# Low parts of the input weights on VectorE in place of GpSimd, and ACT table loads counted by the planner's clock, in a hybrid decoder step on one Trainium2 core

## The chip, the cores and the metric

The kernel runs on one core of one Trainium2 chip. The metric is the device time of one execution in microseconds (us), the median of three runs. The engines are named as the profile names them: PE (TensorE matmul), PEld (its weight loads), DVE (VectorE), ACT (ScalarE), POOL (GpSimd) and SP (SyncE, which here only issues DMAs).

## The reference

One layer of a decoder: two recurrent branches side by side, gated and merged, and then an MLP. It is computed for 512 prompt tokens and for 8 sequences of 4 sample tokens, so that a matrix of activations has 544 columns (552 where the 8 rows of an earlier state are appended). D is 1024, all data are float32.

```python
h = _rmsnorm(x, norm_mix_g)
u = h @ w_in                      # 1024 x 5888: [HGRN2 q,f,i,g | RWKV-7 r,k,v,loras | two gates]
o_a, s_a_new = _hgrn2_branch(...) # 4 heads, state 128x128, chunkwise gated recurrence
o_b, s_b_new = _rwkv7_branch(...) # 8 heads, state 64x64, delta-rule recurrence
x = x + (sigmoid(u_ga) * (o_a @ w_a_out) + sigmoid(u_gb) * (o_b @ w_b_out)) @ w_out
h2 = _rmsnorm(x, norm_mlp_g)
x = x + square(relu(h2 @ w_up)) @ w_down
y = _rmsnorm(x, norm_final_g)
```

The new states and the last normalised row are outputs too.

## The kernel before, in words

**Products.** A large product is made of three float32r products: each operand is split into a high part `hi` and a low part `lo = x - hi`, and hi·hi, lo·hi and hi·lo are added up in PSUM. `split` does this to a block of weights of 128x1024: ACT copies the staged block `st` into `whi`, and a second engine subtracts to make `wlo`. There are three buffers each for `st`, `whi` and `wlo`, so a later DMA of weights (SP's queue) waits until `wlo` of three blocks earlier has been made.

**Units.** The product h @ w_in is cut into 46 units of 128 columns of `w_in` (a token such as `k0`, `f1`, `G8`). A unit is 48 matmuls: two halves of the tokens, three products, 8 blocks of k. `ahead` loads the blocks of the next units and splits them; the variable `loaded` grows by one with each unit. The first 11 blocks are split with DVE, the others with POOL (`NDVE = 11`).

**Lanes.** Between the matmuls of the units stand the steps of the recurrences, in three lanes: LX (the RWKV-7 pairs 0/1, then 2/3: `rw_batch`, `rw_inverse`, `rw_solve`, `rw_affine`, `rw_chain`, `rw_out`), LZ (`low_rank`, `rw_values`, `rw_tokens`) and LY (`hg_head` 0 to 3, then `rw_state`, `rw_sample`, `hg_sample`). A lane is a generator; each `yield` ends one PE step. After every 4 matmuls (`FINE`) or 12 (`QUANT`) `gemm_h` calls `tick`, which goes on with each lane whose last step is ready by the planner's clock.

**The planner's clock.** `Clock` and `Timed` follow the program while it is emitted. Each instruction has a cost by its engine and size, and from the costs come the times at which tiles are ready. So the costs decide after which matmul of which unit a lane's next PE step is emitted. PE runs its instructions in exactly this order (`manual_schedule` for PE); the order on the other engines is set by a scheduler that works on data dependences. `choose` takes the next unit from a list of needed ones or from the gates (`FILL`), by the number of buffers that the lanes hold.

**After the units.** `drain(LX, LZ)` emits what is left in the lanes without matmuls of units between. Then come 8 half units (4 units' worth of matmuls) with `w_b_out`, with the rest of `hg_sample` between them, then those with `w_a_out`, which need the last result of `hg_sample` through DRAM (`oa_d`), then `w_out`, the MLP and the final norm. From `w_out` on PE is fed by large products alone.

Of the kernel before, what the change touches and what calls it, by code (L numbers as in the profile page):

```python
# [8 lines left out]
F32 = mybir.dt.float32  # L9
# [3 lines left out]
AF = mybir.ActivationFunctionType  # L13
ALU = mybir.AluOpType
# [30 lines left out]
PQ, LQ, ZQ, TQ = 0, 0, 1, 0  # L45
POOL_LO = 1
QUANT, FINE = 12, 4
NDVE = 11
NEED = "l0 k0 k1 r0 v0 r1 v1 l1 f0 q0 i0 g0 f1 q1 i1 g1 f2 q2 i2 g2 k2 k3 r2 r3 v2 v3 f3 q3 i3 g3"
FILL = "G8 G10 G2 G1 G3 G7 G13 G4 G11 G15 G9 G12 G5 G6 G14 G0"  # L50
X_WORK = "rw0 rw1"
# [70 lines left out]
class Timed:  # L122


    def __init__(self, eng, name, clock):
        self.eng, self.name, self.clock = eng, name, clock

    def cost(self, fn, out, ops, kw):
        n = 1
        for d in out.shape[1:]:  # L130
            n *= d
        big = max([n] + [int(o.free_size()) for o in ops if hasattr(o, "tensor")])
        if self.name == "PE":
            gemm = len(ops) > 1 and ops[1].dtype == F32R
            switch = 0.12 if gemm != self.clock.gemm else 0.0
            self.clock.gemm = gemm
            if gemm:
                return n / 2400 + 0.013 + switch
            if fn == "transpose":
                return 0.11 * max(n, 32) / 128 + switch  # L140
            return max(n, 32) * (0.00085 if ops[0].shape[-1] >= 128 or n >= 128 else 0.0006) + switch
        if fn == "dma_start":
            return 2.3
        if self.name == "V":
            if fn == "reciprocal":
                return 0.1 + 0.0064 * n
            if fn == "tensor_tensor_scan":
                return 0.1 + 0.0022 * n
            return 0.15 + 0.00106 * big
        if self.name == "A":  # L150
            return 0.17 + 0.0009 * big
        if fn == "tensor_tensor":
            return 0.2 + 0.0025 * big
        return 0.3 + 0.0012 * big
# [25 lines left out]
def hybrid_step(ctx: ExitStack, tc: tile.TileContext, i, o):  # L180
    nc = tc.nc
    clock = Clock()
    V, A, P, T = (Timed(e, n, clock) for e, n in ((nc.vector, "V"), (nc.scalar, "A"), (nc.gpsimd, "P"), (nc.tensor, "PE")))
# [73 lines left out]
    def tt(out, a, b, op, eng=None):  # L257
        (eng or V).tensor_tensor(out=out, in0=a, in1=b, op=op)
# [27 lines left out]
    class W:  # L286
        pass

    def split(st, eng=None):
        w = W()  # L290
        w.hi = pipe.tile([128, 1024], F32R, tag="whi", name=nm("whi"))
        w.lo = pipe.tile([128, 1024], F32R, tag="wlo", name=nm("wlo"), bufs=3)
        act(w.hi, st)
        tt(w.lo, st, w.hi.bitcast(F32), ALU.subtract, eng)
        return w

    def load8(src, c):
# [237 lines left out]
    def column(tok):  # L535
        n = int(tok[1:])
        if tok[0] in "lrkv":
            return B0 + 128 * ({"r": 0, "k": 4, "v": 8, "l": 12}[tok[0]] + n)
        return G0 + 128 * n if tok[0] == "G" else A0 + 512 * "qfig".index(tok[0]) + 128 * n

    need, fill, done, held, plan = NEED.split(), FILL.split(), set(), [0], []
    loaded, weights = {}, {column("l0"): pre}
# [13 lines left out]
    def ahead(c):  # L556

        for n, tok in enumerate(plan[0:3]):
            if tok not in loaded:
                loaded[tok] = load8(i["w_in"][0], column(tok))  # L560
        for tok in plan[0:2]:
            if tok in loaded and column(tok) not in weights:
                weights[column(tok)] = split(loaded[tok], P if len(loaded) > NDVE else V)
        return weights.pop(c)

    def in_unit(c, cuts=(0, HALF, TOK)):
# [30 lines left out]
    for kind in range(2):  # L597
# [3 lines left out]
        w = S(512, F32R, "lwd")  # L601
# [967 lines left out]
    while plan:  # L1569
        tok = plan.pop(0)  # L1570
# [58 lines left out]
    for jp in range(4):  # L1629
        if jp < 3:  # L1630
            wb.append(split(load4(i["w_b_out"][0], 256 * jp + 256)))
        w = wb[jp]
# [20 lines left out]
    for jp in range(4):  # L1653
        w = split(load4(i["w_a_out"][0], 256 * jp))
# [169 lines left out]
    for j in range(8):  # L1824
        st = load8(i["w_down"][0, 3072:4096], 128 * j)
        if j < 8 - NKEEP:
            w = []
# [54 lines left out]
```

## Time and profile before

| | us |
|---|---|
| median of 3 runs (lowest, highest) | 1102.83 (1100.08, 1108.12) |
| the profiled execution's own time | 1101.6 |
| its span, from the first to the last instruction | 1099.9 |

Busy time as a share of the span: PE 87%, PEld 84%, DVE 52%, ACT 37%, POOL 18%. The mean clock granted to PE is 0.937 of full speed. Of the chain of work that ended last, 62% is PE, 15% DVE, 7% DMA, 7% ACT, 4% POOL.

How to read it: PE is in order, so a lane's step that isn't ready holds up the matmuls behind it too. The units and lanes take the first 576 us of the span, the products with `w_b_out` and `w_a_out` go on to about 649 us, and the rest is PE-bound. What a step costs is therefore seen in the idle time of PE ahead of it, in brackets in the rows, with the engine and tile that ended it.

### The profile page before, as it was taken

How to read it: one execution, taken by the hardware profiler on the slowest of the kernel's cores; microseconds unless marked ns; L12 is line 12 of the kernel's file. 1: busy time of each engine (PE TensorE's matmuls, PEld its weight loads, DVE VectorE, ACT ScalarE, POOL GpSimd, SP SyncE). 2: the span in 40 equal slices, each digit the busy share in tenths (PEclk: the TensorE clock that was granted, in tenths of full speed). 3: DMA queues.
4: the chain of work that ended last, by engine and by line, in shares of the span. 5: the costliest groups of instructions: out<-in, count | busy, mean ns of one | idle time of the engine just before them, and what ended most of it. 6: DMA issues, size and time to landing. Idle time of an engine off the chain costs nothing.

```text
span 1099.9 us, 21956 instructions
## 1 busy us (share of the span) xinstructions
PE 957.2 (87%) x9220; PEld 923.6 (84%) x9220; DVE 577.3 (52%) x1135; ACT 404.9 (37%) x761; POOL 198.5 (18%) x335
## 2 busy tenths in 40 slices
PE   5887778798987879779949599999999999999996
PEld 4787767787887878769738599999999999999996
DVE  6464639445766585713566585544432234444533
ACT  7451524546444433433231234334311123332332
POOL 4267443222254442221010000000000000000000
PEclk9798788899998889989968799999999999999998
DMA  8421323221133233341265445332333323233411
GB/s 241 135 85 53 101 69 74 74 60 42 60 100 101 78 93 69 92 121 43 79 185 183 156 127 157 88 97 78 96 87 87 95 78 97 79 104 90 133 39 44
DMA packets 191093, 106.40 MB, mean 97 GB/s; under 512 B 38946, under 2 KB 179048, under 8 KB 190995
## 3 DMA queue, kind: packets, MB, share of 16 engines
q1 hardware_dynamic: 165424, 95.16, 29.6%
q10 hardware_dynamic: 25570, 9.85, 3.5%
q8 instruction: 72, 1.18, 0.4%
q14 instruction: 27, 0.21, 0.1%
HBM read 85.08 MB, written 18.39 MB: 94 GB/s over the span
## 4 chain that ended last, share of the span: by engine, by line
PE 62%; DVE 15%; DMA 7%; ACT 7%; POOL 4%; issue 4%; SPq 1%; ACTq 1%; POOLq 0%; DVEq 0%
PE pd L160 21%; PE full_unit_ps L160 14%; PE in_unit_ps L160 14%; PE half_unit_ps L160 3%; DVE tmp L160 2%; DMA st<-in_w_down_dram 2%; ACT whi L160 1%; POOL lmk L394 1%; DVE wlo L160 1%; ACT L160 1%; DVE X L160 1%; DVE rs L160 1%; DVE bn L160 1%; PE lora_ps L160 1%; SPq L160 1%
## 5 line engine op out<-in xcount | busy, mean ns | idle before, releaser
L160 ACT ACTIVATE whi<-st 128x1024 fp32r<-128x1024 f32 x120 | 126.8, 1056 | 267.9 <-PE pd L160 117.7
L160 DVE TENSOR_TENSOR wlo<-st,whi 128x1024 fp32r<-128x1024 f32 x85 | 104.1, 1225 | 65.9 <-ACT whi L160 65.8
L160 PE MATMUL in_unit_ps<-h_hi,wlo 128*128 128x272 f32 (+3 forms) x736 | 122.2, 302 | 0.0
L160 PE MATMUL in_unit_ps<-h_hi,whi 128*128 128x272 f32 (+3 forms) x736 | 117.7, 304 | 3.5 <-ACT h_hi L160 3.3
L160 PE MATMUL in_unit_ps<-h_lo,whi 128*128 128x272 f32 (+3 forms) x736 | 111.6, 295 | 0.0
L160 PE MATMUL full_unit_ps<-hd,whi 128*128 128x272 f32 (+2 forms) x832 | 109.8, 288 | 0.0
L160 PEld LDWEIGHTS in_unit_ps<-h_hi,whi 128*128 128x128 f32 x736 | 104.8, 200 | 5.4 <-ACT h_hi L160 3.8
L160 PEld LDWEIGHTS in_unit_ps<-h_hi,wlo 128*128 128x128 f32 x736 | 105.3, 197 | 2.0 <-issue 0.3
L160 PEld LDWEIGHTS full_unit_ps<-hd,whi 128*128 128x128 f32 x832 | 106.2, 188 | 0.0
L160 POOL TENSOR_TENSOR wlo<-st,whi 128x1024 fp32r<-128x1024 f32 x35 | 85.8, 2451 | 98.6 <-ACT whi L160 97.4
L160 PEld LDWEIGHTS in_unit_ps<-h_lo,whi 128*128 128x128 f32 x736 | 102.3, 195 | 0.1
L160 POOL TENSOR_SCALAR ys<-ys,ssf 32x512 f32<-32x512 f32 x1 | 1.1, 1087 | 532.8 <-DVE ssf L160 532.8
L160 DVE SCALAR_TENSOR_TENSOR r<-pd,rsb 128x272 f32<-128x272 f32 x64 | 25.2, 436 | 90.5 <-PE pd L160 89.1
L160 PE MATMUL pd<-xgh,wlo 128*128 128x272 f32 x512 | 70.1, 288 | 0.0
L160 PE MATMUL pd<-xgh,whi 128*128 128x272 f32 x512 | 69.8, 288 | 0.0
L160 PE MATMUL pd<-xgl,whi 128*128 128x272 f32 x512 | 69.6, 287 | 0.0
L160 PEld LDWEIGHTS pd<-xgh,wlo 128*128 128x128 f32 x512 | 66.4, 188 | 0.0
L160 PEld LDWEIGHTS pd<-xgh,whi 128*128 128x128 f32 x512 | 66.3, 188 | 0.0
L160 PEld LDWEIGHTS pd<-xgl,whi 128*128 128x128 f32 x512 | 66.2, 188 | 0.0
L160 DVE TENSOR_TENSOR x<-x,full_unit_ps 128x272 f32<-128x272 f32 (+2 forms) x48 | 19.5, 435 | 71.6 <-PE full_unit_ps L160 71.6
L160 PE MATMUL full_unit_ps<-hd,wlo 128*128 128x272 f32 (+2 forms) x416 | 56.5, 288 | 0.0
L160 PEld LDWEIGHTS full_unit_ps<-hd,wlo 128*128 128x128 f32 x416 | 53.8, 188 | 0.0
(414 smaller groups left out, 1558.9 us busy)
## 6 DMA issues: line engine op xcount, KB each, us to landing
st<-in_w_in_dram SPq DMA_DIRECT2D x46, 512.0 KB
st<-in_w_up_dram SPq DMA_DIRECT2D x32, 512.0 KB
st<-in_w_down_dram SPq DMA_DIRECT2D x32, 512.0 KB
gt_d<-gt SPq DMA_DIRECT2D x16, 272.0 KB
st<-in_w_out_dram SPq DMA_DIRECT2D x8, 512.0 KB
gtb<-gt_d SPq DMA_DIRECT2D x8, 272.0 KB
gta<-gt_d SPq DMA_DIRECT2D x8, 272.0 KB
x<-xt_d SPq DMA_DIRECT2D x8, 272.0 KB
```

The lines of the kernel that those rows point to most:

```text
L160: r = real(*a, **kw)
L394: return tc.keep_in_program_order(getattr(nc.gpsimd, name)(*a, **kw))
```

## The change

Two edits. `split` loses its argument for the engine, and `ahead` its test on `NDVE`: the low parts of blocks 12 to 46 of `w_in` are made on DVE, not on POOL. And the planner's cost of an ACT instruction is now 1.3 us higher where its function lies in another table set than the last one, and 0.2 us higher where it also writes a sum (`accum_out`). The second edit changes no instruction, but the order in which PE steps of lanes and units are emitted, and the order of units that `choose` makes.

```diff
-NDVE = 11
...
     def __init__(self, eng, name, clock):
-        self.eng, self.name, self.clock = eng, name, clock
+        self.eng, self.name, self.clock, self.table = eng, name, clock, 0
...
         if self.name == "A":
-            return 0.17 + 0.0009 * big
+            sets = {AF.Tanh: 1, AF.Exp: 1, AF.Sigmoid: 2, AF.Ln: 3, AF.Sqrt: 4}
+            new = sets.get(kw.get("func"), self.table)
+            load, self.table = 1.3 if new != self.table else 0.0, new
+            return 0.17 + 0.0009 * big + load + (0.2 if "accum_out" in kw else 0.0)
...
-    def split(st, eng=None):
+    def split(st):
...
-        tt(w.lo, st, w.hi.bitcast(F32), ALU.subtract, eng)
+        tt(w.lo, st, w.hi.bitcast(F32), ALU.subtract)
...
-                weights[column(tok)] = split(loaded[tok], P if len(loaded) > NDVE else V)
+                weights[column(tok)] = split(loaded[tok])
```

POOL around unit 12, before. `smk`, `bmk` and `mneg` are masks made by `consts3`, `sxl` is the low part of a product that PE sums over a head (`head_sums`).

```order
L394 MEMSET smk 128x64
L160 TENSOR_TENSOR wlo_1462<-st_1329,whi_1461 128x1024
L394 AFFINE_SELECT smk<-smk 32x32 x16
L394 MEMSET bmk 128x8
L394 AFFINE_SELECT bmk<-bmk 32x8 x8
L394 MEMSET mneg 128x1
L394 MEMSET mneg 32x1 x2
L160 TENSOR_TENSOR sxl_1484<-rk_1481,sxh_1483 128x544
```

The same place on POOL, now.

```order
L396 MEMSET smk 128x64
L396 AFFINE_SELECT smk<-smk 32x32 x16
L396 MEMSET bmk 128x8
L396 AFFINE_SELECT bmk<-bmk 32x8 x8
L396 MEMSET mneg 128x1
L396 MEMSET mneg 32x1 x2
L162 TENSOR_TENSOR sxl_1496<-rk_1493,sxh_1495 128x544
```

The block's low part `wlo_1462` no longer stands between the masks and `sxl`; on DVE it stands between two multiplications of the same pair's preparation.

PE at the solve of the pairs 2/3, before. `rw_state` transposes the sample states, `rw_solve_py` is the first step of `rw_solve`.

```order
L160 MATMUL rw_state_ps_5548<-ident,sn_5543 128x128 x4
L160 MATMUL in_unit_ps_5555<-h_hi,whi_5300 128x272 x8
L160 MATMUL in_unit_ps_5555<-h_hi,wlo_5301 128x272 x4
L160 MATMUL rw_state_ps_5585<-ident,sn_5568 128x128 x4
L160 MATMUL in_unit_ps_5555<-h_hi,wlo_5301 128x272 x4
L160 MATMUL in_unit_ps_5555<-h_lo,whi_5300 128x272 x8
L160 MATMUL rw_solve_py_5604<-XT_5573,zb_4550 32x32 x16
L160 MATMUL rw_solve_py_5604<-XT_5573,zb_4790 32x32 x16
L160 MATMUL in_unit_ps_5672<-h_hi,whi_5413 128x272 x8
L160 MATMUL in_unit_ps_5672<-h_hi,wlo_5414 128x272 x4
```

The same place on PE, now.

```order
L162 MATMUL rw_state_ps_5799<-ident,sn_5782 128x128 x4
L162 MATMUL in_unit_ps_5769<-h_hi,wlo_5543 128x272 x4
L162 MATMUL in_unit_ps_5769<-h_lo,whi_5542 128x272 x8
L162 MATMUL rw_solve_py_5818<-XT_5787,zb_4639 32x32 x16
L162 MATMUL rw_solve_py_5818<-XT_5787,zb_4997 32x32 x16
L162 MATMUL rw_state_ps_5858<-ident,sn_5853 128x128 x4
L162 MATMUL rw_solve_px_5869<-TT_5791,YT_5788 32x32 x16
L162 MATMUL rw_solve_px_5869<-TT_5796,YT_5788 32x32 x16
L162 MATMUL rw_sample_ps_5929<-rs_5907 64x64 x8
L162 MATMUL rw_sample_pt_5939<-ident,bd_5920 128x128 x4
L162 MATMUL rw_affine_pw_5946<-KA_5125,TT_5791 64x128 x8
```

Before, 192 matmuls of units (4 units) are left when the solve begins, and stand between its steps; now the last matmul of the last unit stands ahead of it.

PE at the end of `hg_sample`, before. `half_unit_ps` with `whi_6846` is the last block of `w_b_out`, with `whi_7091` the first of `w_a_out`.

```order
L160 MATMUL half_unit_ps_7010<-ol_6668,whi_6846 128x272
L160 MATMUL half_unit_ps_7010<-ol_6674,whi_6846 128x272
L160 MATMUL hg_sample_po_7023<-hs_6468,hs_6469 32x128 x4
L160 MATMUL hg_sample_pt_7050<-ident,hs_6468 128x128
L160 MATMUL half_unit_ps_7097<-oh_7067,whi_7091 128x272
```

The same place on PE, now. `whi_6812` is the last but one block of `w_b_out`, `whi_6898` the last.

```order
L162 MATMUL half_unit_ps_6972<-ol_6689,whi_6812 128x272
L162 MATMUL half_unit_ps_6972<-ol_6695,whi_6812 128x272
L162 MATMUL hg_sample_pt_6985<-ident,hs_6366 128x128
L162 MATMUL half_unit_ps_6997<-oh_6676,whi_6898 128x272
L162 MATMUL half_unit_ps_6997<-oh_6682,whi_6898 128x272
```

Before, `hg_sample_po` and `hg_sample_pt` follow one another behind the last matmul with `w_b_out`; now 36 matmuls stand between the two, and the 48 of the last block behind them.

## Rows read from the trace of the kernel before

**Rows 1.** Busy time by stretch: start:end, length, PE, PEld, DVE, ACT, POOL, PEclk, DMA.

```profile
125.00:488.00 363.00, 298.75 (x3611) 285.41 (x3611) 227.69 (x464) 155.69 (x316) 128.70 (x162) 0.92 0.29 79
```

**Rows 2.** What PE waited for from 125 to 488 us: total, times, longest.

```profile
PE hg_head_pt L160 <- DVE kh L160: 16.3, 4, 7.7
PE hg_head_pt L160 <- DVE hy L160: 16.1, 3, 8.2
PE head_sums_ps L160 <- POOL sxl L160: 6.9, 2, 6.2
PE rw_state_ps L160 <- DMA sn<-in_state_wkv_dram: 6.4, 1, 6.4
PE head_sums_ps L160 <- ACT sxh L160: 5.3, 1, 5.3
```

**Rows 3.** Groups of instructions: count, busy us, mean ns, idle time before and releaser.

```profile
L160 DVE TENSOR_TENSOR wlo<-st,whi 128x1024 fp32r<-128x1024 f32 x85 | 104.1, 1225 | 65.9 <-ACT whi L160 65.8
L160 POOL TENSOR_TENSOR wlo<-st,whi 128x1024 fp32r<-128x1024 f32 x35 | 85.8, 2451 | 98.6 <-ACT whi L160 97.4 <-POOL xi L160 1.0
L160 ACT ACT_TABLE_LOAD x19 | 24.4, 1283 | 2.3 <-PEq L1870 1.5 <-ACT gB L160 0.5
```

**Rows 4.** DVE in order of time, at four places from 132 to 506 us.

```profile
132.99 2.62 DVE L160 TENSOR_TENSOR eb<-kka,b 128x256 f32<-128x256 f32 x1
...
321.38 0.79 DVE L160 SCALAR_TENSOR_TENSOR xm<-d,prm,U 128x544 f32<-128x544 f32 x1
...
328.21 2.84 DVE L160 SCALAR_TENSOR_TENSOR xm<-d,prm,U 128x544 f32<-128x544 f32 x1 [2.87 <-POOL d L160]
...
504.41 2.10 DVE L160 TENSOR_TENSOR s0T<-s0T,rs 128x512 f32<-128x512 f32 x2 [1.04 <-PE rw_sample_pz L160]
```

**Rows 5.** POOL in order of time, 328 us.

```profile
328.13 2.34 POOL L160 TENSOR_TENSOR wlo<-st,whi 128x1024 fp32r<-128x1024 f32 x1
```

**Rows 6.** POOL in order of time, 132 to 146 us.

```profile
132.94 2.39 POOL L160 TENSOR_TENSOR wlo<-st,whi 128x1024 fp32r<-128x1024 f32 x1
...
144.04 1.33 POOL L160 TENSOR_TENSOR sxl<-rk,sxh 128x544 fp32r<-128x544 f32 x1
```

**Rows 7.** The chain that ended last, in order of time, a half unit: start, us, what.

```profile
231.12 3.21 PE in_unit_ps L160 x24
```

**Rows 8.** Busy time of the unit tiles alone, 488 to 542 us.

```profile
488.00:542.00 54.00, 27.83 (x192) 24.79 (x192) 0.00 (x0) 3.14 (x8) 1.00 0.19 64
```

**Rows 9.** Busy time by stretch, columns as in rows 1.

```profile
545.00:575.00 30.00, 14.37 (x188) 9.95 (x184) 18.66 (x61) 10.67 (x23) 2.75 (x9) 0.67 0.56 152
```

**Rows 10.** ACT in order of time, between the two steps of the solve and after.

```profile
489.42 1.21 ACT L160 ACTIVATE YT<-rw_solve_py 32x512 f32<-32x512 f32 x2
...
493.12 1.56 ACT L160 ACTIVATE TT<-rw_solve_px 32x256 f32<-32x256 f32 x4 [0.37 <-PE rw_solve_px L160]
```

**Rows 11.** DVE in order of time, first and last of the norm in `rw_sample`.

```profile
522.36 0.42 DVE L160 TENSOR_TENSOR rs<-rw_sample_pu,rs 128x256 f32<-128x256 f32 x1
...
529.01 0.42 DVE L160 TENSOR_TENSOR rs<-rs,gs 128x256 f32<-128x256 f32 x1
```

**Rows 12.** PE in order of time, two steps of `rw_chain` of pairs 2/3.

```profile
533.72 0.45 PE L160 MATMUL rw_chain_ps<-st,GQ 64*64 64x64 f32 x8
...
534.86 0.40 PE L160 MATMUL rw_chain_ps<-st,GQ 64*64 64x64 f32 x8
```

**Rows 13.** PE in order of time, `rw_out` of pairs 0/1 and of pair 2.

```profile
310.74 2.26 PE L160 MATMUL rw_out_pt<-ident,yo 64*64 64x64 f32 x64
...
560.93 1.97 PE L160 MATMUL rw_out_pt<-ident,yo 64*64 64x64 f32 x32
```

**Rows 14.** PE in order of time, 615 to 625 us.

```profile
615.67 0.45 PE L160 MATMUL hg_sample_pt<-ident,hs 128*128 128x128 f32 x1 [4.71 <-DVE hs L160]
622.50 2.42 PE L160 MATMUL half_unit_ps<-oh,whi 128*128 128x272 f32 x9 [6.38 <-ACT oh L160]
```

**Rows 15.** DVE in order of time, the first step of the second solve.

```profile
462.04 1.53 DVE L160 STREAM_TRANSPOSE XT<-D 32x256 f32<-32x256 f32 x4 [4.15 <-DMA D<-xz_d]
```

## The prediction

> **What bounds the kernel now.** I read the table of busy time by stretch first. From 125 to 488 us, where the lanes of both branches run between the units, PE is busy 299 of 363 us at a granted clock of 0.92 [rows 1], so 64 us are idle. The list of what PE waited for says on what: two of the steps of `hg_head` (`kh`, `hy`) for 16.3 and 16.1 us, the operands of `head_sums` (`sxl`, `sxh`) for 6.9 and 5.3, and a load of states (`sn`) for 6.4 [rows 2]: 51 of the 64 us in five rows. None of these is a wait for weights: no row has PE waiting for `wlo`. PE is in order, so a wait means that a lane's step was emitted before the chain on DVE, ACT and POOL behind it could be done. The engines themselves have room there, DVE with 228 us busy of 363, ACT 156, POOL 129. From 488 to 575 us the units' last 192 matmuls fill the gaps of the solve and the chain of the pairs 2/3 [rows 8]; then comes an uncovered end, 14.4 us busy of 30 at a clock of 0.67 [rows 9], and a second one at 610 to 622 us, where PE waits 4.7 us for the last norm of `hg_sample` and 6.4 us for its way through DRAM [rows 14]. Behind 649 us nothing changes: there PE is fed by large products alone.
>
> I work from the profiled execution, 1101.6 us, which lies 1.2 us below the median of the runs shown.
>
> **Part 1, the low parts.** 35 instructions go from POOL, at 2.451 us each, to DVE, at 1.225 us [rows 3]: 85.8 us less on POOL, 35 x 1.225 = 42.9 us more on DVE. But before, POOL's subtraction also held up DVE. An `xm` of 0.79 us took 2.84 us, and began 0.08 us behind a `wlo` of 2.34 us on POOL [rows 4, 5]. I went through DVE's instructions beside each of the 35: 24 of the 35 have one that is stretched, by 0.6 to 2.2 us over the common time of its form, from the `eb` at 133 us to the `s0T` at 504 us [rows 4], and the stretches add up to 39 us. So DVE gets back about 39 of the 43 us that it takes on, a net 4 us over 450, of which I put 2 us on the path. Bounds: if none of the stretch came back, up to 43 us of DVE work would be new, and at DVE's share of two thirds most of it would queue in front of a lane; if the stretch falls where lanes wait and the new work where DVE idles, up to 10 us are gained.
>
> The Trainium skill has the rule for such a stretch ("SBUF — State Buffer", section on the two separate sides): a GpSimd instruction and a VectorE instruction with two SBUF inputs take one shared pair of ports as an exclusive lock, and the one that comes second stands still for the whole of the other. The `xm` row agrees, a stretch of 2.05 us beside 2.34. The rule also speaks against the change, since `wlo` on DVE has two SBUF inputs and can now be held up by the POOL instructions that stay.
>
> What stays on POOL that is long are the eight `sxl`, 1.33 us each [rows 6]; 8 x 1.3 = 10 us if every one of them met a `wlo`, which 35 instructions of 1.2 us in 450 us will seldom do, so I take under 1 us, inside the 2 above. On the path POOL itself goes away at one place: `sxl` at 144 us stands behind a `wlo` of 2.39 us and 8 us of masks, and PE waits 6.2 us for it [rows 2, 6]. Without the `wlo` it is ready 2.4 us earlier.
>
> **Part 2, the planner's clock.** A table load takes 1.283 us on ACT [rows 3], so the new 1.3 us is what the engine does, and lanes are thought to be ready later. In the order their PE steps stand behind more matmuls of units. A half unit of 24 matmuls takes 3.21 us [rows 7], that is 0.134 us each. The solve of the pairs 0/1 stands behind 996 matmuls in place of 876, that of the pairs 2/3 behind all 2208 in place of 2016. So 192 matmuls, 25.7 us, go from behind the second solve to places in front of it. Where they land in a wait they cost nothing. Wait by wait, with the matmuls between the producer's last PE step and the waiting one:
> - `sxl`, 6.2 us: 24 more matmuls (3.2 us) and 2.4 us from POOL: 5.5 us gone.
> - `kh` of heads 0 to 3: 36, 36, 24, 36 matmuls become 48, 24, 24, 24, a net 24 fewer (-3.2 us). Against that, the stretched `xm` (2.05 us) and the wait of 2.87 us on POOL ahead of it [rows 4] stood in front of head 2's `kh`, the longest of the four, and a like stretch in front of head 1's. I take 4 us gone.
> - `hy`: 48, 48, 60, 48 become 60, 48, 72, 60, so 3 x 1.6 = 4.8 us; and in front of three of them DVE was stretched by about 2 us each, like the `xm` [rows 4], less a `wlo` of 1.2 us: 2.4 us. 7 us gone.
> - `sxh`, 5.3 us: 84 matmuls become 168: 6 us gone, with 0.7 of `sxl` behind it.
> - `sn`, 6.4 us: its DMA now stands behind the DMA of the last gate but one, which ends a unit: I count 4 us for it, 2.4 gone.
>
> Together 25 us, between 10 (if new waits open where none were) and 35. The clock at 0.92 [rows 1] also comes back in part as PE's pauses get fewer: 4 us, between 0 and 10.
>
> What the 192 matmuls hid lies bare now. From the second solve to the last `rw_chain_py` I add up, with what PE still has beside it (`rw_state`, `rw_sample`): `YT` 1.2 us with 0.6 covered, `TT` 1.6 us with 1.2 covered [rows 10], with semaphores 1.5 us; four turns of `rw_affine` 1.5; two turns of `rw_sample_pu` that now stand back to back 1.8; the norm of `rw_sample`, 522.4 to 529.4 us [rows 11], of which some 2.5 us were other work, now in PE's way: 4.5; seven steps of `rw_chain`, at 1.14 us from one to the next when nothing stands between and 0.45 us of PE [rows 12], 7 x 0.7 = 5 us. Sum 14 us. Then the clock: `rw_out` took 2.26 us for 64 matmuls between units and 1.97 us for 32 in the uncovered end [rows 13], 1.74 times as long each. The tail has about 33 us of PE work in small steps; if a third of it runs at the lower level, 33 / 3 x 0.74 = 8 us; I take 7. Bounds of the tail: 8 us (waits overlap `hg_sample`, clock holds) and 38 us (14 us of waits, and all of the work at the lower level, 24).
>
> At the end of `hg_sample`, 36 matmuls (4.8 us) now cover the 4.7 us of the norm, and 48 (6.4 us) the 6.4 us of the way through DRAM [rows 14]. Of 11.1 us I take 8 as gone, since the shorter distances between the steps before it may cost 2 or 3; bounds 0 and 11.
>
> **Sum.** -25 (waits from 125 us to the second solve) + 2 (DVE) - 4 (clock there) + 14 + 7 (bare tail) - 8 (end of `hg_sample`) = -14. 1101.6 - 14 = 1087.6, and I say 1087 us.
>
> **Rivals.**
> - *The tail takes the place of the waits.* The gains come but the second solve is late all the same, or the tail costs 22 us and the end nothing: -25 + 2 + 22 = -1, less 1 to 2 for the clock: 1099 us. For it: the lane of the pairs 2/3 ends the units' part whatever stands before it. Against it: the first step of that solve was done on DVE at 463.6 us [rows 15], and PE came to it only at 488, where its last 192 matmuls of units begin [rows 8], so it has over 20 us of slack.
> - *Slower: the bare tail at the lower clock.* Mechanism: from the solve of the pairs 2/3 to `rw_out` PE runs small steps with pauses, the granted clock falls as at 545 to 575 us [rows 9], and each step takes 1.74 times as long. Then the tail costs 38 us, and with the low end of the gains (-10 - 4 + 2) and nothing at the end: +26, less 10 that the end and the clock still give: 1118 us. It decides as soon as the tail costs more than the waits give back, 33 us with the values above. Against it: in the same steps of the pairs 0/1 there is much to fill, so no row shows the tail bare.
> - *DVE becomes the bound.* The stretch doesn't come back, 43 us of new DVE work lie in front of lanes and a quarter of it is felt, 11 us more than I take, with 2 us fewer gains from the clock: about 1101 us. Against it: the stretched rows.
>
> **How the numbers follow.** 1% of the time, 11 us, is about what a measurement tells from no change. Forecast 0.55, with its own range 1074 to 1097: of it 0.46 faster, 0.09 the same. Tail in place of waits 0.22: 0.04 faster, 0.18 the same. Slower tail 0.16: 0.14 slower, 0.02 the same. DVE bound 0.07: 0.04 the same, 0.03 slower. Sums: faster 0.50, the same 0.33, slower 0.17. The range 1070 to 1114 takes in the ends of the gains (35) and leaves out the worst tail.
>
> **What would show it.** Right: no `wlo` on POOL and no stretched `xm`; the rows for `hy` and `sxh` shrink by 7 and 6 us; the second solve within 5 us of 488 us with all units done; the waits of PE from there to `w_b_out` higher by about 14 us, at a granted clock near 0.8; at the end no wait of 6 us for `oh`. Wrong: `kh` and `hy` waits that stay, behind a `wlo` in DVE's queue; a tail at a clock below 0.7; or PE waiting more than 8 us at `rw_state` for `sn`.

## The result, and the profile after

The changed kernel takes 1073.65 us (median of 4 runs, 1071.51 to 1077.67) beside 1102.98 us for the kernel before on the same chip: a ratio of 0.9733, with a 95% interval from 0.9687 to 0.978. Forecast were 1087 us. The sign and the range held; the gain of 29 us is twice the 14 us of the sum. The profiled execution took 1071.5 us with a span of 1069.8, 30.1 less than the span before, and the rows below are compared with it.

The table of busy time by stretch of the changed kernel (columns as in [rows 1]):

```profile
125.00:488.00 363.00, 329.60 (x4162) 315.21 (x4162) 240.22 (x514) 173.33 (x347) 62.19 (x138) 0.97 0.33 89
488.00:575.00 87.00, 51.08 (x651) 40.85 (x647) 49.60 (x140) 17.82 (x39) 2.90 (x9) 0.74 0.36 105
575.00:623.00 48.00, 46.26 (x357) 45.39 (x356) 39.25 (x88) 15.66 (x22) 0.00 (x0) 0.96 0.49 156
```

The first row answers to [rows 1]: PE is busy for 330 of 363 us where it was 299, at a granted clock of 0.97 in place of 0.92. POOL has 62 us of work there, half of before, and DVE 240 in place of 228. The second row is the bare tail: 51 of 87 us, at 0.74. In the third, the end of `hg_sample`, PE is nearly full.

What PE waited for in the changed kernel from 125 to 478 us:

```profile
PE rw_batch_pt L162 <- ACT KA L162: 8.7, 6, 2.4
PE hg_head_pt L162 <- DVE kh L162: 7.1, 3, 4.2
PE rw_state_ps L162 <- DMA sn<-in_state_wkv_dram: 3.6, 1, 3.6
PE in_unit_ps L162 <- DVE xq L162: 2.8, 1, 2.8
PE head_sums_ps L162 <- POOL sxl L162: 2.7, 1, 2.7
PE hg_head_pt L162 <- DVE hy L162: 1.6, 1, 1.6
```

Against [rows 2], `hy` falls from 16.1 to 1.6 us, `kh` from 16.3 to 7.1, `sxl` from 6.9 to 2.7, `sn` from 6.4 to 3.6, and `sxh` has no row left. Two rows are new or larger: `KA`, the steps of `rw_batch` that stand close together, and `xq`.

The tail, in the same view from 471 to 559 us:

```profile
PE half_unit_ps L162 <- DMA ox<-ob_d: 8.3, 1, 8.3
PE rw_sample_pt L162 <- DVE rs L162: 5.7, 1, 5.7
PE hg_sample_pl L162 <- DVE hs L162: 5.5, 1, 5.5
PE rw_out_pt L162 <- DVE rs L162: 5.2, 1, 5.2
PE hg_sample_pn L162 <- DVE s0A L162: 2.7, 1, 2.7
```

PE in order of time at four places (start, length, idle time before in brackets):

```profile
470.61 1.20 PE L162 MATMUL rw_solve_py<-XT,zb 32*32 32x32 f32 x64
...
558.32 0.59 PE L162 MATMUL half_unit_ps<-oh,whi 128*128 128x272 f32 x1 [8.35 <-DMA ox<-ob_d]
...
584.78 0.27 PE L162 MATMUL hg_sample_pt<-ident,hs 128*128 128x128 f32 x1
...
592.81 2.43 PE L162 MATMUL half_unit_ps<-oh,whi 128*128 128x272 f32 x10 [1.74 <-ACT oh L162]
```

The second solve begins at 470.6 us with all units done. Before it began at 487.9 with 192 unit matmuls (25.7 us) still to come, so by there 17.2 + 25.7 = 42.9 us are gained. The first half unit came at 574.7 before and comes at 558.3 now: the tail gives back 26.6 us. At the end of `hg_sample` the last transposition has no wait in place of 4.71 us and `oh` 1.74 in place of 6.38 [rows 14]; from the first half unit of `w_b_out` to the first of `w_a_out` it is 34.5 us in place of 47.8, a gain of 13.3. 42.9 - 26.6 + 13.3 = 29.6 of the 30.1 us. Behind that point nothing moved (477.4 us before, 477.0 now).

PE's busy and idle time, cut at these points, says what the three parts are made of. The stretches are from 125 us to the second solve, on to the first half unit, and on to the first product with `w_a_out` (columns as in [rows 1]). Before:

```profile
125.00:487.85 362.85, 298.60 (x3603) 285.26 (x3601) 227.54 (x463) 155.65 (x315) 128.70 (x162) 0.92 0.29 79
487.85:574.68 86.83, 70.34 (x1100) 60.12 (x1099) 43.82 (x131) 29.63 (x66) 10.22 (x19) 0.89 0.33 96
574.68:622.50 47.82, 33.83 (x242) 31.14 (x242) 29.80 (x64) 7.30 (x12) 0.00 (x0) 0.79 0.50 161
```

The changed kernel:

```profile
125.00:470.61 345.61, 313.48 (x3784) 300.69 (x3783) 232.12 (x494) 163.93 (x324) 59.63 (x131) 0.97 0.34 92
470.61:558.32 87.71, 52.55 (x915) 42.20 (x914) 46.46 (x141) 23.92 (x57) 5.46 (x16) 0.75 0.28 77
558.32:592.81 34.49, 30.71 (x238) 28.62 (x239) 24.26 (x55) 7.49 (x12) 0.00 (x0) 0.88 0.56 182
```

Idle is the length less PE's busy time. The busy time is given without the 192 matmuls (25.7 us) that changed sides, so it is the same work on both sides, and most of a difference in it is the granted clock: by the trace PE was busy at the lower of its two levels for 34.3, 11.0 and 10.7 us of the three parts before, and for 16.3, 25.6 and 6.1 now. The lower level is half of the higher one there, so half of each difference, -9.0, +7.3 and -2.3 us, is what the clock did.

| in us | forecast | measured | PE idle | PE busy |
|---|---|---|---|---|
| to the second solve | -25 + 2 - 4 = -27 | -42.9 | 64.3 to 32.1: -32.1 | 298.6 to 287.8: -10.8 |
| the bare tail | 14 + 7 = +21 | +26.6 | 16.5 to 35.2: +18.7 | 44.6 to 52.6: +7.9 |
| the end of `hg_sample` | -8 | -13.3 | 14.0 to 3.8: -10.2 | 33.8 to 30.7: -3.1 |

The groups of instructions that answer to [rows 3]:

```profile
L162 DVE TENSOR_TENSOR wlo<-st,whi 128x1024 fp32r<-128x1024 f32 x120 | 147.1, 1225 | 91.2 <-ACT whi L162 91.1
...
L162 ACT ACT_TABLE_LOAD x21 | 26.9, 1283 | 2.3 <-PEq L1872 1.4 <-ACT gB L162 0.5
```

All 120 low parts are on DVE at the same 1.225 us, and no group of POOL has `wlo`. DVE stood idle for 91 us ahead of them, for ACT's high part: where it waits, it comes to them before their data are there. DVE's whole busy time is 581.5 us, 4.2 more than before, as the prediction's net of 4 us has it.

### The profile page after: what moved, and what is told of

Same layout as the page of the kernel before. It is cut to its first block, busy times and chain, and to the rows that moved or that the text cites. A ratio compares the mean times of both kernels' runs of the same rounds, so it can differ in the third digit from the quotient of the medians.

```text
span 1069.8 us, 21969 instructions
## 1 busy us (share of the span) xinstructions
PE 950.7 (89%) x9220; PEld 918.6 (86%) x9220; DVE 581.5 (54%) x1170; ACT 408.7 (38%) x763; POOL 122.4 (11%) x300
## 4 chain that ended last, share of the span: by engine, by line
PE 71%; DVE 11%; ACT 5%; DMA 5%; POOL 4%; issue 2%; SPq 1%; ACTq 0%; DVEq 0%; POOLq 0%
PE pd L162 22%; PE full_unit_ps L162 17%; PE in_unit_ps L162 16%; PE half_unit_ps L162 5%; DVE tmp L162 2%; POOL lmk L396 1%; ACT whi L162 1%; DMA bn<-zb_d 1%; PE lora_ps L162 1%; PE rw_chain_py L162 1%; DVE wlo L162 1%; DVE rs L162 1%; ACT L162 1%; PE rw_affine_pw L162 1%; DVE bn L162 1%
## 5 line engine op out<-in xcount | busy, mean ns | idle before, releaser
L162 DVE TENSOR_TENSOR wlo<-st,whi 128x1024 fp32r<-128x1024 f32 x120 | 147.1, 1225 | 91.2 <-ACT whi L162 91.1
L162 PE MATMUL in_unit_ps<-h_hi,whi 128*128 128x272 f32 (+3 forms) x736 | 114.5, 299 | 6.1 <-ACT h_hi L162 3.3
L162 PE MATMUL in_unit_ps<-h_hi,wlo 128*128 128x272 f32 (+3 forms) x736 | 119.9, 298 | 0.0
L162 PEld LDWEIGHTS in_unit_ps<-h_hi,whi 128*128 128x128 f32 x736 | 102.0, 195 | 7.9 <-ACT h_hi L162 3.7
L162 PE MATMUL half_unit_ps<-oh,whi 128*128 128x272 f32 x128 | 24.9, 314 | 12.1 <-DMA ox<-ob_d 8.3
```

The lines of the kernel that those rows point to most:

```text
L162: r = real(*a, **kw)
```

## Experiments: engine or order

The change does two things at once, it moves 35 low parts and it moves the order of PE. Four kernels take them apart: each edit alone, and each order of PE with either engine. In the last two the planner books the low part on one engine while another executes it, so that PE has the same instructions in the same order as the kernel that it is built from; the order on the other engines follows from the data. In all that follows the ratios are to runs of the kernel before on the same chip; 0.01 is 11 us. The changed kernel's own ratio is 0.9733, and 0.9721 when it was timed again below; 0.9727 is used.

**Low parts on DVE alone, old cost of ACT.**

```diff
-            sets = {AF.Tanh: 1, AF.Exp: 1, AF.Sigmoid: 2, AF.Ln: 3, AF.Sqrt: 4}
-            new = sets.get(kw.get("func"), self.table)
-            load, self.table = 1.3 if new != self.table else 0.0, new
-            return 0.17 + 0.0009 * big + load + (0.2 if "accum_out" in kw else 0.0)
+            return 0.17 + 0.0009 * big
```

> The low parts of blocks 12 to 46 on DVE as in the changed kernel, but the planner keeps its old cost of ACT (no table loads, no sums). In the order that comes out, the second solve stands behind all 2208 matmuls of the units, as in the changed kernel (before: 2016), so the order is moved by the planner booking the low parts on DVE. Theory A (the later places of the lanes' steps carry the gain, whatever edit causes them): 1074 to 1080 us, as the changed kernel. Theory B (the ACT cost carries the planner's part, as the prediction said, and the move of engine only the stretched DVE instructions): 1088 to 1095 us. Theory C (the engine carries nothing, only the table loads): 1100 us.

Measured: 1078.19 us (1073.2 to 1085.71), ratio 0.9783 (0.973 to 0.9836). That is within theory A's range: 24 of the 30 us are there without the table loads, and so is the order. By itself, the booking on DVE puts all 2208 matmuls ahead of the second solve.

**New cost of ACT alone, low parts on POOL.** The edit is the one above the other way round, on the kernel before.

> The new ACT cost in the planner alone, the low parts of blocks 12 to 46 on POOL as before. The second solve stands behind 2028 matmuls (before 2016, changed kernel 2208), so the order hardly moves. Theory A (later places carry the gain): 1098 to 1103 us, no change. Theory B (the ACT cost carries the planner's part of the gain): 1085 to 1092 us.

Measured: 1096.68 us (1093.5 to 1100.86), ratio 0.9948 (0.9926 to 0.997), a gain of 6 us. It lies between the ranges of both theories. The table loads move the steps by 0 to 36 matmuls, and they are not what put the units ahead of the solve. The prediction said that they were. Yet so small a move takes much of PE's idle time: up to the second solve, which comes at 476.2 us with 180 matmuls left, it falls from 64.3 to 47.8 us, 13 us are gained by there, and the tail gives 7 of them back.

**Order of the changed kernel, low parts on POOL.**

```diff
+    PV = Timed(nc.gpsimd, "V", clock)
...
-                weights[column(tok)] = split(loaded[tok])
+                weights[column(tok)] = split(loaded[tok], PV if len(loaded) > 11 else V)
```

> The changed kernel's order of PE, instruction for instruction, but the low parts of blocks 12 to 46 are made on POOL (the planner still books them on DVE). Theory A (the order carries most): the stretched DVE instructions are back, 39 us of DVE, and a few us of them are felt: 1078 to 1086 us. Theory B2 (the gain is the end of the stretched DVE instructions and of POOL's long subtraction on the path, and the order only moves waits about): 1095 to 1103 us.

Measured: 1097.08 us (1094.46 to 1106.02), ratio 0.9956 (0.9932 to 0.998). Theory A falls, theory B2's range holds it. PE at the second solve, and what it waited for up to there:

```profile
494.96 1.20 PE L162 MATMUL rw_solve_py<-XT,zb 32*32 32x32 f32 x64
```

```profile
PE rw_batch_pt L162 <- ACT KA L162: 10.2, 5, 4.6
PE head_sums_ps L162 <- POOL sxl L162: 9.6, 3, 3.8
PE rw_batch_pa L162 <- DVE bv L162: 5.0, 1, 5.0
PE hg_head_pt L162 <- DVE hy L162: 3.8, 1, 3.8
...
PE hg_head_pt L162 <- DVE kh L162: 2.9, 3, 1.6
```

**Order of the kernel before, low parts on DVE.**

```diff
+    VP = Timed(nc.vector, "P", clock)
...
-                weights[column(tok)] = split(loaded[tok], P if len(loaded) > NDVE else V)
+                weights[column(tok)] = split(loaded[tok], VP if len(loaded) > NDVE else V)
```

> The order of PE of the kernel before, instruction for instruction, but the low parts of blocks 12 to 46 are made on DVE (the planner still books them on POOL). Theory A (the order carries most): the stretched DVE instructions go, the waits of hy and kh shrink by some 2 us each, at the same clock: 1090 to 1098 us, with the second solve at 475 to 483 us of the span. Theory B2 (the engine carries the gain): 1074 to 1082 us. A third outcome, 1100 or more: DVE's own new 43 us stand in front of the lanes, which only the later places make up for.

Measured: 1084.8 us (1073.81 to 1087.13), ratio 0.9817 (0.976 to 0.9875), between the two theories. PE at the second solve, and what it waited for from 125 to 488 us:

```profile
463.26 1.20 PE L160 MATMUL rw_solve_py<-XT,zb 32*32 32x32 f32 x64
```

```profile
PE hg_head_pt L160 <- DVE hy L160: 10.6, 3, 5.8
PE hg_head_pt L160 <- DVE kh L160: 7.8, 3, 3.2
PE head_sums_ps L160 <- POOL sxl L160: 6.8, 2, 5.1
```

The four corners, as ratio to the kernel before and as the time at which PE comes to the second solve:

| | low parts on POOL | low parts on DVE | the engine alone |
|---|---|---|---|
| order of before (192 unit matmuls left) | 1, at 487.9 us | 0.9817, at 463.3 | -20 us; -24.6 at the solve |
| order of after (none left) | 0.9956, at 495.0 | 0.9727, at 470.6 | -25 us; -24.4 at the solve |
| the order alone, with 25.7 us of units moved | -5 us; +7.1 - 25.7 = -18.6 | -10 us; +7.3 - 25.7 = -18.4 | |

By the ratios the engine is worth 20 to 25 us and the order 5 to 10; with intervals of 0.2 to 0.6% either way, it isn't shown whether they add up exactly. Of its 18.5 us at the solve the order keeps 5 to 10 at the end, since the tail takes back more than the end of `hg_sample` gives.

That the engine comes out at 24.6 and 24.4 us at the solve is closer than one execution each can say. The profiled execution with the order of before and the low parts on DVE took 1073.8 us, the fastest of its four by 11 us, and the changed kernel's second profiled execution, further down, comes to the solve 3.8 us later than its first. And what stands behind the two is not the same. Up to the solve, with the new order and the low parts on POOL, then with the old order and the low parts on DVE:

```profile
125.00:494.96 369.96, 324.25 (x3791) 309.73 (x3790) 228.65 (x460) 161.95 (x323) 134.19 (x165) 0.94 0.31 86
125.00:463.26 338.26, 298.03 (x3606) 285.34 (x3604) 224.61 (x495) 156.90 (x315) 59.85 (x132) 0.95 0.31 85
```

The order alone, on POOL, takes 18.5 us off PE's idle time (64.3 to 45.7) and nothing off its busy time (298.6 + 25.7 to 324.3; 34.4 us of it are at the lower level, as before). The engine, in the new order, takes 13.6 off the idle time (45.7 to 32.1) and 10.8 off the busy time (324.3 to 313.5), 7.0 in the second execution. In the old order it takes 24.0 off the idle time (64.3 to 40.2) and next to nothing off the busy time. So in part the two edits remove the same waits. The order alone brings `kh` from 16.3 to 2.9 us and `hy` from 16.1 to 3.8; the engine alone brings them to 7.8 and 10.6. In the new order the engine ends other waits, `bv` (5.0 us) and most of `sxl` (9.6 to 2.7), and `kh` is longer again (7.1). The `sxl` wait hardly moves by the engine alone, although the `wlo` ahead of it on POOL is gone; why is open.

## Experiments: why the engine is worth that much

DVE's busy time is nearly the same with the low parts on either engine (576 us on POOL, 581 on DVE, in the new order), and still PE is 24 us earlier. Either the stretch of DVE's instructions [rows 4, 5] costs more per microsecond than work that DVE takes on, or it is not the stretch: POOL's queue is also shorter, and the low parts come sooner. Three kernels put spare work on POOL into the changed kernel, for the same 35 blocks, that nobody needs. It writes `st` when the low part has been made, so `st` is free for the next DMA a little later. PE's order is that of the changed kernel in all three, and the three have the same order on DVE and POOL as one another (26 of DVE's 1170 instructions stand elsewhere than in the changed kernel).

```diff
-    def split(st):
+    def split(st, spare=False):
...
         tt(w.lo, st, w.hi.bitcast(F32), ALU.subtract)
+        if spare:
+            nc.gpsimd.tensor_tensor(out=st, in0=st, in1=w.hi.bitcast(F32), op=ALU.subtract)
...
-                weights[column(tok)] = split(loaded[tok])
+                weights[column(tok)] = split(loaded[tok], len(loaded) > 11)
```

> The changed kernel with its order of PE instruction for instruction, and for blocks 12 to 46 one more subtraction on POOL that nobody needs: st = st - whi, 128x1024, 2.45 us, after the low part has been made on DVE. Theory L (POOL's two-input instructions stop DVE inside the lanes' chains): the stretched DVE instructions are back, some 35 us in all, and most of the 23 us between the changed kernel (1073.7) and the same order with the low parts on POOL (1097.1): 1087 to 1097 us. Theory Q (POOL's own queue: the lanes' POOL instructions stand behind the long one): also 1085 to 1097 us, but the same with the single-input twin. Theory W (the low parts themselves come too late when POOL makes them, 2.45 in place of 1.23 us): 1073 to 1077 us, since here they come from DVE.

Measured: 1106.06 us (1104.35 to 1107.41), ratio 1.0022 (1.0003 to 1.004): 32 us more than the changed kernel, more than any theory had it, and no faster than the kernel before. Theory W falls, since here the low parts come from DVE; and with the low parts on POOL no wait of PE was for `wlo`.

The second has one input in place of two:

```diff
-            nc.gpsimd.tensor_tensor(out=st, in0=st, in1=w.hi.bitcast(F32), op=ALU.subtract)
+            for _ in range(2):
+                nc.gpsimd.tensor_scalar(out=st, in0=st, scalar1=1.0, scalar2=0.0, op0=ALU.mult, op1=ALU.add)
```

> As the run before, but POOL's spare work on each of the blocks 12 to 46 has one input: two times st = st * 1 + 0, 128x1024, about 1.2 us each, so POOL is as busy as with the subtraction. Theory L (two-input instructions stop DVE): no stretched DVE instruction beside them, 1073 to 1078 us. Theory Q (POOL's queue): 1085 to 1097 us, as with two inputs. Theory W: 1073 to 1077 us.

Measured: 1094.52 us (1093.23 to 1096.02), ratio 0.9917 (0.9887 to 0.9948): 21 us more. By the expectation that speaks for the queue; but theory L had assumed that one input stops nobody, and the trace says otherwise. DVE and POOL of this kernel in order of time:

```profile
305.73 1.55 DVE L162 TENSOR_TENSOR yo<-yo,gs 128x512 f32<-128x512 f32 x1
```

```profile
305.70 2.50 POOL L299 TENSOR_SCALAR st<-st 128x1024 f32<-128x1024 f32 x2 [9.14 <-DVE gs L162]
```

A multiplication that takes 0.69 us elsewhere takes 1.55, from the start of POOL's first instruction to behind its end. So the runs had not yet told the two apart, and a third kernel was made, whose work reads nothing:

```diff
-                nc.gpsimd.tensor_scalar(out=st, in0=st, scalar1=1.0, scalar2=0.0, op0=ALU.mult, op1=ALU.add)
+                nc.gpsimd.memset(st, 0.0)
```

> As the two runs with spare work on POOL, with the same order on PE, DVE, ACT and SP, but the work reads nothing: two times memset of st, 128x1024, about 1.05 us each (a memset of 128x512 takes 0.53 us), 74 us of POOL in all, against 80 with one input and 87 with two. Theory L (POOL's reading instructions stop DVE): the stretch of DVE beside them (37 us with two inputs, 23 with one) is near zero, and so is the cost: 1074 to 1079 us. Theory Q (POOL's queue, and the later release of st): 1089 to 1095 us, since POOL is almost as busy as with one input (1094.5). In between, the share of either is read from it: with 0.9 us per us of stretch, 1075 plus 0.9 times the stretch is L alone.

Measured: 1080.89 us (1078.07 to 1081.76), ratio 0.9769 (0.9739 to 0.98), just above theory L's range and far below theory Q's: 5 us more than the changed kernel by the ratios, with POOL busy for 67 us on it (70 instructions of 0.96 us). One tile of DVE shows why (count: shortest/median/longest in ns). With two inputs on POOL:

```profile
L162 DVE TENSOR_TENSOR X<-xq,E x28: 410/421/2604, 137.3 to 461.6; 128x256 f32<-128x256 f32 x28
```

With none:

```profile
L162 DVE TENSOR_TENSOR X<-xq,E x28: 408/420/458, 135.9 to 435.1; 128x256 f32<-128x256 f32 x28
```

With one, DVE in order of time at an instruction of this tile, and POOL beside it:

```profile
240.24 1.26 DVE L162 TENSOR_TENSOR X<-xq,E 128x256 f32<-128x256 f32 x1
241.42 1.26 DVE L162 TENSOR_TENSOR E<-hb 128x256 f32<-128x256 f32 x1
```

```profile
240.07 2.34 POOL L299 TENSOR_SCALAR st<-st 128x1024 f32<-128x1024 f32 x2 [1.54 <-DVE wlo L162]
```

The median is 0.42 us; only the long ones differ. The longest takes 2.60 us beside a POOL instruction of 2.51 us with two inputs, the one above 1.26 beside one of 1.16 with one input (about what is left of POOL's instruction and their own time; the next one, `E`, waits in the same way for POOL's second), and none is over 0.46 with the memset. Going through all of DVE's instructions with two inputs that began while a spare one ran, 19 of 45 are stretched by over 0.15 us with two inputs on POOL, 24 of 59 with one, and 0 of 73 with none.

The Trainium skill says just this ("SBUF — State Buffer", section "Who interferes with whom": a DVE instruction with two SBUF inputs contends with a GpSimd instruction that reads SBUF, not with one that only writes it). The three runs agree, with 2.60, 1.26 and 0.46 us. The prediction had told the rule with two inputs on VectorE and any GpSimd instruction, and the expectation of the second run with two inputs on both; the one is too wide, the other too narrow.

Added up from 125 to 576 us, for each instruction of DVE that began while the spare work ran, its time less the common time of its form in the changed kernel:

| POOL's spare work | POOL busy, us | stretch of DVE, us | time over the changed kernel, us |
|---|---|---|---|
| none | 0 | 0 | 0 |
| memset | 67.2 | 3.0 | 5 |
| one input | 80.4 | 22.2 | 21 |
| two inputs | 86.8 | 35.6 | 32 |

From the second row to the last, 32.6 us of stretch cost 27.9 us, 0.86 us for each. The third row lies on that line: 4.6 + 0.86 x 19.2 = 21.1. (The subtraction also reads `whi`, and so holds its buffer longer; the work with one input doesn't, and lies on the same line.) POOL's occupation alone, and the later release of `st`, are at most the 5 us of the memset, or 6 to 7 if they grow with POOL's busy time. So theory L holds for most of it, with a share of theory Q of 1 to 7 us. The price holds waits and clock together: from the memset to two inputs, PE's idle time ahead of the second solve grows from 34.3 to 52.2 us and its busy time from 319.8 to 327.5.

And what the added work on DVE costs shows in two kernels with the same order of PE and the same load on POOL: with the low parts on POOL the ratio is 0.9956, with the low parts on DVE and the same subtraction as spare work 1.0022. That is 7 us for 43 us of DVE work, 0.17 us for each. The two are not quite alike (in the one PE waits for POOL's result, in the other nobody does), so this is an estimate from two runs. But the signs are clear: -32 us for the stretch and POOL, +7 for the work. That they give the -25 of the corner table follows from the way they are taken, and is no test.

## Experiments: the bare tail

The changed kernel's data for the second solve were there long before PE came to it. All the instructions for `XT` (first and last start in the middle):

```profile
L162 DVE STREAM_TRANSPOSE XT<-D x8: 390/410/438, 191.9 to 439.9; 32x256 f32<-32x256 f32 x8
```

They end at 440.3 us, and the solve is emitted for 470.6. If the planner takes less time for the inverse, the solve stands earlier and units are left to fill the tail. Three kernels scale the planner's costs of DVE inside the second inverse.

```diff
-            return 0.15 + 0.00106 * big
+            return (0.15 + 0.00106 * big) * self.clock.inv
...
-        yield from rw_inverse(g)
+        for got in rw_inverse(g):
+            clock.inv = 1.0
+            yield got
+            clock.inv = 0.4 if g else 1.0
+        clock.inv = 1.0
```

> The changed kernel, with the planner's costs of DVE times 0.4 inside the inverse of the pairs 2/3 alone, so that their solve stands behind 2100 matmuls of the units in place of all 2208 (its data were ready 30 us before PE came to it), and 108 matmuls (14.5 us) lie between its steps and those of rw_affine. Theory A (they fill waits of the bare tail, 35 us there now, and the clock of 0.74 rises): 1060 to 1068 us. Rival (hg_sample's steps are emitted 48 matmuls later among the half units, and the wait for oh of some 6 us returns; the tail's longest waits, the norms, stay): 1070 to 1077 us.

Measured: 1066.6 us (1064.84 to 1068.46), ratio 0.966 (0.9623 to 0.9697).

> The same with the factor 0.6: the solve stands behind 2136 matmuls, 72 of them (9.6 us) in the tail; hg_sample's steps stand 48 matmuls later, as with 0.4. Theory A: 1063 to 1070 us, between the changed kernel and the run before. Rival: 1070 to 1078 us.

Measured: 1072.45 us (1072.07 to 1076.6), ratio 0.9724 (0.9678 to 0.9771).

> The changed kernel with the planner's costs of DVE times 0.2 inside the inverse of the pairs 2/3: the solve stands behind 2076 matmuls (2100 with 0.4, 2136 with 0.6, 2208 in the changed kernel), 132 of them (17.7 us) in the tail. Its data are ready early enough by 30 us of slack. Theory A (more cover for the tail): 1062 to 1066 us, at or below the 1066.6 with 0.4. Rival (what ends last there is hg_sample and the way of rw_out's result through DRAM, which no cover of the solve shortens): 1066 to 1070 us.

Measured: 1072.35 us (1071.78 to 1073.46), ratio 0.97 (0.9666 to 0.9733).

Only 0.4 was ahead, so it was run again beside the changed kernel, on one chip.

> The changed kernel, unaltered, timed again on the same chip and against the same runs of before as the kernel with the earlier solve: 1071 to 1078 us, a ratio to before of 0.971 to 0.977. It is the base from which the earlier solve is judged.

Measured: 1073.95 us (1071.71 to 1075.28), ratio 0.9721 (0.9697 to 0.9745).

> The kernel with the factor 0.4 (the solve of the pairs 2/3 behind 2100 matmuls) again, beside the changed kernel. If the 7 us by which it was ahead are real: 1064 to 1069 us, a ratio to before of 0.964 to 0.969, with an interval that ends below the changed kernel's. If they were the spread between runs (the kernels with 0.6 and 0.2 were at 1072): 1070 to 1076 us.

Measured: 1065.87 us (1063.54 to 1067.27), ratio 0.965 (0.9627 to 0.9674). The intervals don't meet: this kernel is 8 us faster than the changed one and 38 us faster than the one before. PE in order of time in this run:

```profile
443.66 1.20 PE L163 MATMUL rw_solve_py<-XT,zb 32*32 32x32 f32 x64
...
518.21 1.15 PE L163 MATMUL half_unit_ps<-oh,whi 128*128 128x272 f32 x2 [9.78 <-ACT oh L163]
...
577.14 0.45 PE L163 MATMUL hg_sample_pt<-ident,hs 128*128 128x128 f32 x1 [4.14 <-DVE hs L163]
...
583.94 1.73 PE L163 MATMUL half_unit_ps<-oh,whi 128*128 128x272 f32 x6 [6.35 <-ACT oh L163]
```

The solve is 27 us earlier than in the changed kernel and the first half unit 40 us, but the last transposition of `hg_sample` only 7.6 us, and it waits again, as does `oh` (6.35 us), the wait that the rival had said would return. The rest of the 40 us lies as waits among the half units, at a granted clock of 0.77 from 488 to 575 us.

So with 0.4 theory A had the time right but not the place, and with 0.6 and 0.2 the times are outside its ranges. Counted as above, with 0.134 us for each matmul of units that is left at the solve:

| planner's factor | unit matmuls left | gained by the solve, us | tail and end of `hg_sample` without them, us |
|---|---|---|---|
| 1 (the changed kernel) | 0 | 0 | 122.2 |
| 0.6 | 72 | 6.1 | 128.3 |
| 0.4, first and second execution | 108 | 11.2, 12.5 | 127.4, 125.8 |
| 0.2 | 132 | 13.0 | 133.4 |

On balance the units left fill no waits: they take waits out of the tail and put as many among the half units, and without their own time the tail and the end together are longer than in the changed kernel, in all four executions. What the factor 0.4 gains stands ahead of the solve, where PE's idle time falls from 32.1 to 25.7 us; in part that is 16 small matmuls (`rw_state`, `hg_head`) and a wait for `sn` that now come behind it. The factors 0.2 and 0.6 lose behind the solve what they gain ahead of it, and their last transposition of `hg_sample` stands at 584.2 and 586.0 us, as in the changed kernel. Why 0.4 loses least is open. One execution for each number, and the changed kernel's second execution was itself 4 us later at the solve than its first, so a single difference of that size says little.

## Why the prediction was right, and where not

**The sum.** The sign and the range held, and the sum had half of the gain. The tail came out 5.6 us dearer and the end of `hg_sample` 5.3 us cheaper than said; that these two cancel is luck. The miss of 15 us lies ahead of the second solve: -42.9 us where -27 were said.

**The DVE term, +2 us, is the step that failed.** The prediction found the stretch, counted it rightly (39 us; the spare subtractions bring back 36) and then set it against the 43 us of new work as if a microsecond of either were worth the same on the path. The runs price the first at 0.86 and the second at about 0.17, so the term has the wrong sign. The reading that fits: the stretch falls on whatever DVE has in hand, from 125 us on mostly a lane's chain that PE waits for next, while the low part for the next unit can be done in any gap ahead of its unit. No run tests that reading by itself. With the 12 us that the wait-by-wait list put down to POOL and the stretch (2.4 of `sxl`, about 7 of `kh`, 2.4 of `hy`), the prediction's engine part was -10 us. It measured -20 to -25, in the new order 13.6 us of waits and 7 to 11 of PE's own busy time. The bound "up to 10 us are gained" was too near as well. The low parts on DVE were not held up, as the prediction feared; the longest took 1.35 us.

**The waits, -25 us.** Largely right in place, wrong in size and cause. `hy` lost 14.5 us where 7 were taken, `kh` 9.2 where 4 were, `sxl` 4.2 (5.5), `sxh` 5.3 (6), `sn` 2.8 (2.4). PE's idle time as a whole fell by 32.1 us. The two rows that were far off have stretched instructions in front of them, and the engine alone takes 8.5 us of `kh` and 5.5 of `hy`; but the order alone takes 13.4 and 12.3, so their miss belongs to neither by itself. Five us of new waits for `KA` and 3 for `xq` came with the closer steps.

**What sets the order.** The prediction put the later places down to the table loads. The runs with one edit alone show that it is the booking of the low parts on DVE in the planner's clock, 35 times 1.2 us that it had not had there. The prediction read the places from the order itself, so its count of matmuls was right: by its own steps the order was to give 13 us of waits (the matmuls at `sxl`, `kh` and `hy`, then `sxh` and `sn`) by the solve, and it gave 18.5.

**The second solve** was to come within 5 us of 488 us with all units done. It came at 470.6: the engine brought it 24.4 us forward, the order 7.1 back.

**The clock, -4 us.** The granted clock rose from 0.92 to 0.97 over 363 us, and PE's busy time for the same work fell by 10.8 us (7 in the second execution) where 4 were taken. PE was busy at the lower level for 34.3 us before, 34.4 with the new order alone, 30.9 with the new engine alone, and 16.3 (25.1 in the second execution) with both. Why it takes both is open.

**The bare tail, +21 us.** Measured 26.6: 18.7 of idle time where 14 were taken, and 7.9 of busy time for 7, at a clock of 0.75 where "near 0.8" was expected. So it is the waits that were too low. The missing row is `half_unit` waiting 8.35 us for `ox`, the way of the result of `rw_out` through DRAM, 3.6 us before. The other long waits are the norms (5.7, 5.5 and 5.2 us).

**The end of `hg_sample`, -8 us**, gave 13.3, of it 10.2 of idle time; the other 3.1 are the clock, which the prediction had not priced there. Both waits of [rows 14] went as said (no wait, and 1.74 us), and nothing of the 2 or 3 us kept back for shorter distances was lost; the clock in this part rose from 0.79 to 0.88.

**The rivals.** The tail alone did what the slower rival feared in part, it took 26.6 of 42.9 us. It does not decide, because the gain ahead of it was half as large again. DVE as the bound did not come: its new work is the cheapest item in the account. (The slower rival's threshold of 33 us leaves out the terms for DVE and the clock; with them it is 35.)

## What to carry to other kernels

Busy time that one engine loses to another engine's instruction is not worth the same as busy time that a scheduler can place (here 0.86 and 0.17 us for each), so price the two apart even where they sum to zero. Before moving work off an engine for its speed, look at which of its neighbour's instructions are far over the common time of their form, and at what stands beside them. And where one edit changes both an engine and a planner's costs, run the new order with the old engine and the old order with the new one: two more kernels show what each does, and whether the two take the same waits. Read such a split from PE's idle and busy time, and look where the profiled execution lies among the runs of its kernel before trusting its last microseconds.

## What the runs showed of the hardware that was not expected

A POOL instruction with one input stops DVE's two-input instructions as one with two inputs does, until about the end of that instruction: 1.26 us for an `X` of 0.42 beside a `TENSOR_SCALAR` of 1.16. A memset on POOL stops none of them (0 of 73). But beside a memset some DVE instructions with a single input were longer; DVE and POOL in the kernel with memsets:

```profile
342.88 1.08 DVE L162 TENSOR_SCALAR al<-al,prm 128x544 f32<-128x544 f32 x1
```

```profile
342.71 0.95 POOL L299 MEMSET st<- 128x1024 f32 x1
```

This `al` takes 0.49 us elsewhere. The Trainium skill has it among the instructions that can use both pairs of ports ("SBUF — State Buffer", section "Who interferes with whom"), and the row agrees. Of the 14 instructions with one input that began beside a spare memset, 6 were stretched, by 2.8 us in all: five of six `TENSOR_SCALAR` and the one `COPY`, and none of the other seven (`TENSOR_REDUCE`, `STREAM_TRANSPOSE`, `RECIPROCAL`).
